# Masking the diagonal block of a stick-breaking attention: a product that adds -1e30 on the matrix engine, or an affine selection on GpSimd

## The chip, the cores and the metric

The kernel runs on one core of one Trainium2 chip. The metric is the device time of one execution in microseconds; lower is better. Times in the profile are microseconds unless ns is written.

## What is computed

One layer on 1024 tokens of width 1024: a norm, one wide projection, two branches (stick-breaking attention with 8 heads of 64, and an RWKV-7 time mix), a gated merge, an output projection and a SwiGLU feed-forward. The change is in the attention, whose reference is, cut to what matters:

```python
for i in range(S // 128):                       # blocks of 128 queries
    z = einsum(q_block, k[:kv_len]) * scale     # kv_len = (i + 1) * 128
    strict = s_idx < t_idx                      # a query sees earlier tokens only
    log_fail = where(strict, log_sigmoid(-z), 0.0)
    after = cumsum(log_fail, reverse=True) - log_fail
    w = where(strict, exp(log_sigmoid(z) + after), 0.0)
    out = w @ v[:kv_len]
```

In numbers rather than logarithms: nb = sigmoid(-z) is the chance that a key does not take the stick, and it counts as 1 where the mask forbids the key. The running product of nb from the last key backwards is what the kernel calls its scan; differences of that product are the weights w.

## The kernel before, in words

Nothing in the code says in which order an engine works. Each operation is recorded with an estimated cost, and a list scheduler in Python (`schedule`) then plays the program through with these costs and fixed latencies between engines, gives out buffers, and writes one order per engine. On the chip each engine works through its order and waits on semaphores. All instructions carry the line L528, the line that issues them, so the profile is read by the names of tiles. The scheduler prefers steps of the running stage and fills holes in TensorE's order with "filler": the projections of the next pair of heads and the gate projections (`gate_tiles`), whose products are named d_d<-big_h. Its cost of a GpSimd operation without an entry of its own is 150 + 2.1 ns per element of a partition; that of the mask's product is 107 ns.

The attention works on 4 pairs p of heads, 2 heads h in each, and 4 double blocks j of two query rows (s = 0, 1), so on 64 rows of 128 queries. A row (`head`) goes through these steps:

- TensorE: for each piece of up to 512 keys two products into a PSUM tile e_e, keys times the high part of the queries (e_e<-b_kst,b_qst) and times the low part (e_e<-b_kst,b_ql). In the piece that ends on the diagonal a third product stands between them: identity times mask in bf16 (e_e<-bf_bf,bf_bf), which adds -1e30 where a key is not earlier than the query. Every product first loads its 128 columns of weights (PEld rows).
- ScalarE (ACT): the sigmoid of the piece, b_nb<-e_e.
- VectorE (DVE): one scan over the whole row, b_nb<-b_nb, 128 to 1024 elements wide.
- TensorE: transposes of the 128x128 blocks of the scanned row (c_c<-cst_cst,b_nb); ScalarE and VectorE split them into b_wt; then the products with the values (y_y<-b_wt,b_vhl), and ScalarE and VectorE finish the head's output (q_q, b_osb).

GpSimd (POOL) has little to do in this stage: for each pair, two MEMSETs of b_ql, and for the values COPYs of a few columns and two TENSOR_TENSORs (b_vt). After the attention come the last gate projections, then the merge (`merge`), whose first products are d_d<-b_orw.

Of the kernel before, what the change touches and what calls it, by code (L numbers as in the profile page):

```python
# [8 lines left out]
BF16 = mybir.dt.bfloat16  # L9
AF = mybir.ActivationFunctionType  # L10
ALU = mybir.AluOpType
# [4 lines left out]
P = 128  # L16
# [21 lines left out]

PC_BG, PC_MU, PC_W0, PC_A0, PC_KK, PC_KA, PC_RK, PC_LW, PC_LB, PC_N = 0, 16, 30, 34, 38, 42, 46, 50, 54, 58

CC_ID, CC_CEN, CC_ONE, CC_MA, CC_DM, CC_TI, CC_SC, CC_N = 0, 128, 256, 384, 512, 640, 896, 1408

# [546 lines left out]
def hybrid_block(tc, x, w_in, consts, params, rows, ups, gup, w_sb, w_rw, w_o, w_fg, w_fu, w_fd, out):  # L591
    b = Block(tc, {a.tensor.name for a in (x, w_in, consts, params, rows, ups, gup, w_sb, w_rw, w_o, w_fg, w_fu, w_fd)})
    nc = b
    T = b.t
    with ExitStack() as es:
        b.open(es)
        b.cls("cst", 1, CC_DM)
        b.cls("par", 1, PC_N)
        b.cls("small", 3, 16)
        b.cls("tiny", 4, 4)  # L600
        b.cls("ss", 8, 4)
        b.cls("carry", 5, 1)
        b.cls("pl", 3, 8)
        b.cls("bf", 2, P)
        b.cls("sp", 3, CH)
        b.cls("q", 4, 256)
        b.cls("big", 4, 4 * S)
        for n in ("raw", "whi", "wlo"):
            b.cls(n, 2, S)
        b.cls("b", NB, 1040, halves=True)  # L610
        for n, k in (("d", 2), ("e", 2), ("c", 2), ("y", 2)):
            b.cls(n, k, H, psum=True)

        cst, par = T("cst", [P, CC_DM]), T("par", [P, PC_N])
        b.xin = []
        for m in range(8):
            b.xin.append(T("b", [P, D], F32, "x"))
            nc.sync.dma_start(b.xin[m], x[m * P : m * P + P, :])
            if m == 0:
                nc.sync.dma_start(cst, consts[:, 0:CC_DM])  # L620
                b.gbc = T("b", [P, D])
                nc.sync.dma_start(b.gbc, rows[0:1, :].broadcast_to([P, D]))
            if m == 3:
                b.w_lora = [b.load(w_in[24], [P, KT, P])]
                nc.sync.dma_start(par, params)
            if m == 5:
                b.w_lora.append(b.load(w_in[25], [P, KT, P]))
        b.ident = cst[:, CC_ID : CC_ID + P]
        b.cen = cst[:, CC_CEN : CC_CEN + P]
        b.ones = cst[:, CC_ONE : CC_ONE + P]  # L630
        b.mask_a = cst[:, CC_MA : CC_MA + P]
        b.tinit = consts[:, CC_TI : CC_TI + 256]
        b.scanm = consts[:, CC_SC:CC_N]
        b.eps = T("small", [P, 2])
        nc.gpsimd.memset(b.eps[:, 0:1], RMS_EPS)
        nc.gpsimd.memset(b.eps[:, 1:2], GN_EPS)
        b.identb = T("bf", [P, P], BF16)
        nc.gpsimd.tensor_copy(b.identb, b.ident)
        b.dmask = T("bf", [P, P], BF16)
        dm = T("q", [P, P])  # L640
        nc.sync.dma_start(dm, consts[:, CC_DM : CC_DM + P])
        nc.gpsimd.tensor_copy(b.dmask, dm)
        b.om = T("small", [P, 14])
        nc.gpsimd.tensor_scalar(out=b.om, in0=par[:, PC_MU : PC_MU + 14], scalar1=-1.0, scalar2=1.0, op0=ALU.mult, op1=ALU.add)
        b.oka = T("small", [P, 4])
        nc.gpsimd.tensor_scalar(out=b.oka, in0=par[:, PC_KA : PC_KA + 4], scalar1=-1.0, scalar2=1.0, op0=ALU.mult, op1=ALU.add)
        b.pc = lambda col: par[:, col : col + 1]

        b.gsc = [b.scratch([P, S], f"gsc{j}") for j in range(16)]
        b.orw_d = [b.scratch([P, S], f"orw{p}") for p in range(PAIRS)]  # L650
        b.x2_d = b.scratch([S, D], "x2d")
        b.w_in, b.w_sb, b.w_rw = w_in, w_sb, w_rw
        b.ngate = 0

        b.steady = STEADY[0]
        norm_in(b)
        lora(b, ups, gup)
        b.steady = STEADY[1]
        rwkv(b)
        b.steady = STEADY[2]  # L660
        attention(b)
        b.steady = STEADY[3]
        merge(b)
        b.steady = True
        output(b, x, w_o, rows)
        ffn(b, w_fg, w_fu, w_fd, rows, out)
        b.issue()


def norm_in(b):  # L670
    nc = b.nc
    T = b.t
    b.hT = tuple([T("big", [P, 4, S], F32R, "h") for q in range(2)] for i in range(2))
    b.table("natural_log_exp_and_others")
    def scale(m):
        xs = T("b", [P, D], F32, "xs")
        return xs, b.rstd([b.xin[m]], xs)

    ahead = [scale(0), scale(1)]
    for m in range(8):  # L680
        xs, r = ahead.pop(0)
        nc.vector.scalar_tensor_tensor(out=xs, in0=b.xin[m], scalar=r, in1=b.gbc, op0=ALU.mult, op1=ALU.mult)
        if m + 2 < 8:
            ahead.append(scale(m + 2))
        b.to_channels(("e", "c"), xs, m, b.hT)
        if m in (2, 4):
            w = b.w_lora[m // 2 - 1]
            hi, lo = T("b", [P, KT, P], F32R), T("b", [P, KT, P], F32R)
            nc.scalar.copy(hi, w)
            nc.gpsimd.tensor_tensor(out=lo, in0=w, in1=hi, op=ALU.subtract)  # L690
            b.w_lora[m // 2 - 1] = hi, lo
# [432 lines left out]
def head(b, kst, qst, ql, vhl, ends, h, j, oh, ol):  # L1124

    nc = b.nc
    T = b.t
    rs = slice(h * CH, h * CH + CH)  # L1130
    nb2 = 2 * j + 2
    wh, wl = ([T("b", [P, min(4, nb2 - 4 * g), 256], F32R, "wt") for g in range((nb2 + 3) // 4)] for _ in range(2))
    for s in range(2):
        i = 2 * j + s
        kv = (i + 1) * P
        qs = slice(i * P, i * P + P)
        nb = T("b", [P, S], F32, "nb")
        for c0 in range(0, kv, H):
            n = min(H, kv - c0)
            z = T("e", [P, H])  # L1140
            ks = slice(c0, c0 + n)
            diag = c0 + n == kv
            nc.tensor.matmul(z[:, :n], lhsT=qst[:, qs], rhs=kst[:, ks], start=True, stop=False)
            if diag:
                nc.tensor.matmul(z[:, n - P : n], lhsT=b.identb, rhs=b.dmask, start=False, stop=False, skip_group_check=True)
            nc.tensor.matmul(z[:, :n], lhsT=ql[:, qs], rhs=kst[:, ks], start=False, stop=True)
            nc.scalar.activation(nb[:, ks], z[:, :n], AF.Sigmoid, scale=-0.125)
        rev = nb[:, 0:kv][:, ::-1]
        nc.vector.tensor_tensor_scan(out=rev, data0=rev, data1=rev, initial=1.0, op0=ALU.mult, op1=ALU.bypass)
        for b0 in range(0, i + 1, 4):  # L1150
            nblk = min(4, i + 1 - b0)
            tp = T("c", [P, 4, P])
            for q in range(nblk):
                nc.tensor.transpose(tp[:, q, :], nb[:, (b0 + q) * P : (b0 + q + 1) * P], b.ident)
            dsl = (slice(None), slice(0, nblk), slice(s * P, s * P + P))
            b.split(wh[b0 // 4][dsl], wl[b0 // 4][dsl], tp[:, :nblk, :])
    o = T("y", [P, 256])
    for kb in range(nb2 - 1, -1, -1):
        first, last = kb == nb2 - 1, kb == 0
        cs = slice(P, 256) if first else slice(0, 256)  # L1160
        g, k = kb // 4, kb % 4
        pairs = [(o[:, cs], vhl[g][:, k, h].rearrange("p a c -> p (a c)"), wh[g][:, k, cs])]
        pairs.append((o[0:CH, cs], vhl[g][:, k, h, 0, :], wl[g][:, k, cs]))
        for n, (out, v, w) in enumerate(pairs if first else reversed(pairs)):
            nc.tensor.matmul(out, lhsT=v, rhs=w, start=first and n == 0, stop=last and n == 1, skip_group_check=True)
    ob = T("q", [P, 256])
    for s in range(2):
        ss = slice(s * P, s * P + P)
        nc.scalar.activation(ob[rs, ss], o[CH:P, ss], AF.Identity, bias=ends[rs, 2 * j + s : 2 * j + s + 1])
    nc.vector.tensor_tensor(out=ob[rs, :], in0=ob[rs, :], in1=o[0:CH, :], op=ALU.add)  # L1170
    osl = slice(j * 256, j * 256 + 256)
    b.split(oh[rs, osl], ol[rs, osl], ob[rs, :])
# [348 lines left out]
def layout(i):  # L1521
# [6 lines left out]
    def cols(v):  # L1528
# [12 lines left out]
        np.eye(P) - blk / CH,  # L1541
        blk,
        np.concatenate([s[:, None] < t[None], s[:, None] <= t[None]], 1),
        np.where(np.arange(P)[None, :] >= np.arange(P)[:, None], -1e30, 0.0),
        (np.arange(32)[None, None, :] == 4 * np.arange(8)[None, :, None] + lane).reshape(P, 256),
        np.broadcast_to(np.arange(H)[None] % CH > 0, (P, H)),
    ]
# [28 lines left out]
```

## Time and profile before

| | |
|---|---|
| median of 3 runs | 1660.45 us (1658.56 to 1661.47) |
| the profiled execution's own time | 1659.71 us |
| its span in the trace | 1657.9 us |
| TensorE busy | 1603.0 us, 97% of the span |
| VectorE, ScalarE, GpSimd busy | 68%, 43%, 12% |
| attention in the trace | from about 541 us (first scan) to 787 us (last product with the values) |

The span is what the trace shows from its first to its last instruction; 1.8 us of the execution's own time lie around it. A busy share is an average over stages with different limits.

### The profile page before, as it was taken

The page shows a single profiled execution, that of the slowest core. Times are in us where ns is not written, and L with a number is a line of the kernel's source. Part 1 is how long each engine was busy: PE and PEld are TensorE (multiplying, and loading weights), DVE is VectorE, ACT ScalarE, POOL GpSimd, SP SyncE. Part 2 cuts the span into 40 slices and gives each one's busy share as a digit, 9 for nine tenths or more (in the row PEclk, how much of TensorE's full clock was granted, in tenths as well). Part 3 has the DMA queues.
Part 4 walks back from the last instruction along what each step waited for, and adds up shares of the span by engine and source line. Part 5 has one row for each costly group of instructions (what it writes and reads, how often), then busy time and mean ns, then how long its engine had stood idle before and what let it go on. Part 6 is the DMA issues. An engine that isn't in the chain of part 4 may idle for free.

```text
span 1657.9 us, 23575 instructions
## 1 busy us (share of the span) xinstructions
PE 1603.0 (97%) x8876; PEld 1273.8 (77%) x8876; DVE 1124.1 (68%) x1999; ACT 718.0 (43%) x1403; POOL 206.6 (12%) x344
## 2 busy tenths in 40 slices
PE   6999999999999999999999999999999999999998
PEld 5777776776777777777787788888888888888886
DVE  6567789668784877878248446766666666778484
ACT  7532334433334656566433434333233322455352
POOL 2021232512313010000015120000000000000000
PEclk9999999999999999999999999999999999999999
DMA  6533222242320000001644501233332332774455
GB/s 217 201 88 91 78 80 79 75 137 72 99 77 34 32 26 14 26 26 39 214 135 142 195 39 58 89 96 106 110 107 97 127 95 96 276 270 141 137 167 178
DMA packets 107108, 180.96 MB, mean 109 GB/s; under 512 B 42353, under 2 KB 43505, under 8 KB 106993
## 3 DMA queue, kind: packets, MB, share of 16 engines
q1 hardware_dynamic: 106992, 179.44, 33.1%
q8 instruction: 70, 1.15, 0.3%
q14 instruction: 46, 0.37, 0.1%
HBM read 129.86 MB, written 47.45 MB: 107 GB/s over the span
## 4 chain that ended last, share of the span: by engine, by line
PE 74%; DVE 17%; ACT 4%; issue 3%; DMA 2%; POOL 0%; SPq 0%; DVEq 0%; ACTq 0%; POOLq 0%
PE d_d L528 31%; PE e_e L528 17%; PE c_c L528 15%; PE y_y L528 10%; DVE q_q L528 6%; DVE b_nb L528 3%; ACT b_qst L528 1%; DVE b_wt L528 1%; DVE wlo_wlo L528 1%; DVE b_sv L528 1%; ACT whi_whi L528 1%; DVE b_nx L528 1%; ACT b_wt L528 1%; DVE b_kst L528 1%; DMA b_b<-rows 0%
## 5 line engine op out<-in xcount | busy, mean ns | idle before, releaser
L528 PE MATMUL d_d<-big_h,whi_whi 128*128 128x512 f32 x1280 | 431.5, 408 | 3.7 <-DVE b_kst L528 2.8
L528 PEld LDWEIGHTS d_d<-big_h,whi_whi 128*128 128x128 f32 x1280 | 234.7, 189 | 52.0 <-issue 6.3
L528 PE MATMUL d_d<-big_h,wlo_wlo 128*128 128x512 f32 x640 | 260.3, 407 | 0.0
L528 PEld LDWEIGHTS d_d<-big_h,wlo_wlo 128*128 128x128 f32 x640 | 120.7, 189 | 24.0 <-issue 1.9
L528 DVE TENSOR_TENSOR wlo_wlo<-raw_raw,whi_whi 128x1024 fp32r<-128x1024 f32 (+1 forms) x60 | 70.6, 1177 | 40.0 <-ACT whi_whi L528 38.6
L528 ACT CAST whi_whi<-raw_raw 128x1024 fp32r<-128x1024 f32 (+1 forms) x60 | 55.9, 933 | 92.5 <-PE d_d L528 82.5
L528 DVE TENSOR_TENSOR q_q<-b_nl,q_q 128x2 f32<-128x2 f32 (+30 forms) x248 | 85.6, 345 | 11.0 <-PE y_y L528 2.7
L528 DVE TENSOR_TENSOR_SCAN b_nb<-b_nb 128x128 f32<-128x128 f32 (+3 forms) x64 | 87.5, 1395 | 1.0
L528 POOL TENSOR_SCALAR sp_sp<-b_sv,pl_pl 64x64 f32<-64x64 f32 x120 | 58.1, 485 | 117.7 <-DVE b_sv L528 110.8
L528 DVE TENSOR_REDUCE q_q<-q_q 128x1 f32<-128x2 f32 (+30 forms) x248 | 62.1, 250 | 6.7
L528 PE MATMUL d_d<-b_wd,big_act 128*128 128x512 f32 x264 | 66.6, 395 | 0.0
L528 PE MATMUL e_e<-b_wd,big_act 128*128 128x512 f32 x264 | 66.6, 394 | 0.0
L528 ACT CAST b_wd<-b_wraw 128x512 fp32r<-128x512 f32 x71 | 42.2, 620 | 53.2 <-DVE b_wraw L528 22.7
L528 DVE TENSOR_TENSOR b_wd<-b_wraw,b_wd 128x512 fp32r<-128x512 f32 x71 | 46.7, 686 | 23.4 <-ACT b_wd L528 23.4
L528 PEld LDWEIGHTS d_d<-b_wd,big_act 128*128 128x128 f32 x264 | 49.6, 188 | 11.8
L528 PEld LDWEIGHTS e_e<-b_wd,big_act 128*128 128x128 f32 x264 | 49.6, 188 | 11.8
L528 PE MATMUL c_c<-cst_cst,b_nb 128*128 128x128 f32 x288 | 47.9, 280 | 9.2 <-DVE b_wt L528 4.5
L528 ACT COPY b_xv<-c_c 64x64 f32<-64x64 f32 x64 | 13.3, 208 | 92.1 <-DVE b_xv L528 46.6
L528 ACT CAST b_wt<-c_c 128x512 fp32r<-128x512 f32 (+2 forms) x96 | 43.9, 481 | 21.0 <-PE c_c L528 19.9
L528 DVE TENSOR_TENSOR b_wt<-c_c,b_wt 128x512 fp32r<-128x512 f32 (+2 forms) x96 | 50.0, 547 | 4.5 <-ACT b_wt L528 3.8
L528 PEld LDWEIGHTS c_c<-cst_cst,b_nb 128*128 128x128 f32 x288 | 32.6, 140 | 23.9 <-DVE b_wt L528 12.2
L528 PE MATMUL c_c<-b_wd,big_act 128*128 128x512 f32 x198 | 50.6, 395 | 0.0
(651 smaller groups left out, 3558.0 us busy)
## 6 DMA issues: line engine op xcount, KB each, us to landing
raw_raw<-w_in SPq DMA_DIRECT2D x42, 512.0 KB, 3.4
raw_raw<-w_fg SPq DMA_DIRECT2D x22, 512.0 KB, 3.5
raw_raw<-w_fu SPq DMA_DIRECT2D x22, 512.0 KB, 4.0
b_wraw<-w_fd SPq DMA_DIRECT2D x22, 512.0 KB, 5.0
act<-b_u SPq DMA_DIRECT2D x40, 256.0 KB, 3.4
b_x<-x SPq DMA_DIRECT2D x16, 512.0 KB, 6.3
raw_araw<-act SPq DMA_DIRECT2D x14, 512.0 KB, 4.3
whi_araw<-act SPq DMA_DIRECT2D x14, 512.0 KB, 4.9
```

Of the source, the lines that this page charges most:

```text
L528: getattr(getattr(self.real, op.engine), op.method)(**kw)
```

## The change: what it does

The third product is gone, and with it the mask tile, the bf16 identity, the two conversions and the transfer that made them at the start, and the columns of the constants that held the mask. Instead, after the sigmoids of a row, GpSimd runs one AFFINE_SELECT in place on the diagonal block of b_nb (128x128, float32): it keeps an element where query minus key is positive and writes 1.0 elsewhere. The scan of the row now waits for it.

```diff
-            diag = c0 + n == kv
             nc.tensor.matmul(z[:, :n], lhsT=qst[:, qs], rhs=kst[:, ks], start=True, stop=False)
-            if diag:
-                nc.tensor.matmul(z[:, n - P : n], lhsT=b.identb, rhs=b.dmask, start=False, stop=False, skip_group_check=True)
             nc.tensor.matmul(z[:, :n], lhsT=ql[:, qs], rhs=kst[:, ks], start=False, stop=True)
             nc.scalar.activation(nb[:, ks], z[:, :n], AF.Sigmoid, scale=-0.125)
+
+        own = nb[:, kv - P : kv]
+        nc.gpsimd.affine_select(out=own, in_=own, pattern=[[-1, P]], compare_op=ALU.is_gt, fill=1.0, base=0, channel_multiplier=1)
         rev = nb[:, 0:kv][:, ::-1]
         nc.vector.tensor_tensor_scan(out=rev, data0=rev, data1=rev, initial=1.0, op0=ALU.mult, op1=ALU.bypass)
...
-        b.identb = T("bf", [P, P], BF16)
-        nc.gpsimd.tensor_copy(b.identb, b.ident)
-        b.dmask = T("bf", [P, P], BF16)
-        dm = T("q", [P, P])
-        nc.sync.dma_start(dm, consts[:, CC_DM : CC_DM + P])
-        nc.gpsimd.tensor_copy(b.dmask, dm)
```

The scheduler is not touched, but it plays a different program, so the orders change between the attention's first score products and its last product with the values. Ahead of that stretch TensorE's order is the same, and behind it too, but for the number of filler products in between.

GpSimd's order at the start of the attention, before. The sp_sp are the last of the RWKV chain, b_r the last output of that branch, b_ql the low part of the queries of pair 1, pl_pl and b_vt the values of pair 1:

```order
L528 COPY pl_pl_5328<-b_tmp_3453 128x4
L528 TENSOR_TENSOR b_v_2529<-b_tmp_3453 128x512
L528 TENSOR_TENSOR b_r_2433<-b_r_2433 128x512
L528 MEMSET b_ql_5671 64x1024
L528 MEMSET b_ql_5673 64x1024
L528 MEMSET b_vt_5883 128x1
L528 COPY pl_pl_5991<-b_vt_5883 128x4
L528 TENSOR_TENSOR b_vt_5883<-b_vt_5883 128x512
```

and the same place now, from the same two rows on:

```order
L528 TENSOR_TENSOR b_v_2523<-b_tmp_3447 128x512
L528 TENSOR_TENSOR b_r_2427<-b_r_2427 128x512
L528 AFFINE_SELECT b_nb_5517<-b_nb_5517 128x128
L528 AFFINE_SELECT b_nb_5520<-b_nb_5520 128x128
L528 AFFINE_SELECT b_nb_5570<-b_nb_5570 128x128
L528 AFFINE_SELECT b_nb_5576<-b_nb_5576 128x128
L528 AFFINE_SELECT b_nb_5597<-b_nb_5597 128x128
L528 AFFINE_SELECT b_nb_5639<-b_nb_5639 128x128
L528 MEMSET b_ql_5671 64x1024
L528 MEMSET b_ql_5673 64x1024
L528 AFFINE_SELECT b_nb_5688<-b_nb_5688 128x128
L528 AFFINE_SELECT b_nb_5718<-b_nb_5718 128x128
```

The selections of the first rows stand directly behind the TENSOR_TENSOR on b_r, and the MEMSETs of b_ql have moved behind six of them.

TensorE's order in pair 0, second head, from just behind the score products of the row of 384 keys down to the transposes of that row, before (the 384-key row is b_nb_6547; d_d_6507 is filler):

```order
L528 MATMUL e_e_6544<-b_kst_5492,b_qst_5776 128x512
L528 LDWEIGHTS bf_bf_145
L528 MATMUL e_e_6544<-bf_bf_294,bf_bf_145 128x128
L528 MATMUL c_c_6549<-cst_cst_136,b_nb_6531 128x128
L528 MATMUL e_e_6544<-b_kst_5492,b_ql_5673 128x512
L528 MATMUL c_c_6552<-cst_cst_136,b_nb_6535 128x128 x2
L528 MATMUL d_d_6507<-big_h_186,wlo_wlo_6253 128x512
L528 MATMUL e_e_6563<-b_kst_5492,b_qst_5776 128x512
L528 MATMUL e_e_6563<-b_kst_5492,b_ql_5673 128x512
L528 MATMUL d_d_6507<-big_h_186,whi_whi_6241 128x512
L528 MATMUL e_e_6571<-b_kst_5492,b_qst_5776 128x128
L528 MATMUL c_c_6575<-cst_cst_136,b_nb_6547 128x128 x2
```

and now, from the same place on; the row of 384 keys is b_nb_6585 here, and its first transpose stands behind two more products of 512 columns (one filler, one score product) that follow the last row shown:

```order
L528 MATMUL e_e_6581<-b_kst_5486,b_qst_5745 128x512
L528 MATMUL e_e_6581<-b_kst_5486,b_ql_5673 128x512
L528 MATMUL d_d_6528<-big_h_167,whi_whi_6266 128x512
L528 MATMUL c_c_6590<-cst_cst_136,b_nb_6563 128x128
L528 MATMUL d_d_6528<-big_h_173,whi_whi_6266 128x512
L528 MATMUL e_e_6598<-b_kst_5486,b_qst_5745 128x512
L528 MATMUL e_e_6598<-b_kst_5486,b_ql_5673 128x512
L528 MATMUL c_c_6605<-cst_cst_136,b_nb_6566 128x128 x2
L528 MATMUL e_e_6612<-b_kst_5486,b_qst_5745 128x128
L528 MATMUL e_e_6612<-b_kst_5486,b_ql_5673 128x128
L528 MATMUL d_d_6528<-big_h_167,wlo_wlo_6279 128x512
L528 MATMUL d_d_6528<-big_h_184,whi_whi_6266 128x512
```

The mask product and its weight load are gone, and more filler stands between a row's scores and its transposes. At the start of the attention the four score products of the rows of 384 and 512 keys now stand directly in front of the first row's transpose; before, they stood behind it. In return less filler is left for the end: between the last product with the values and the first d_d<-b_orw stood 96 products d_d<-big_h, and now 75.

## Rows read from the trace of the kernel before

**Rows 1.** The page: span; busy time, share and instructions of each engine; and TensorE's busy share in 40 slices.

```profile
span 1657.9 us, 23575 instructions
PE 1603.0 (97%) x8876; PEld 1273.8 (77%) x8876; DVE 1124.1 (68%) x1999; ACT 718.0 (43%) x1403; POOL 206.6 (12%) x344
PE   6999999999999999999999999999999999999998
```

**Rows 2.** Two stretches, the attention and all that follows: length, busy time of PE, PEld, DVE, ACT and POOL (instructions), granted clock of TensorE as a share of full speed, DMA share, GB/s.

```profile
541.00:787.00 246.00, 231.58 (x1354) 183.27 (x1353) 190.14 (x262) 152.59 (x345) 16.54 (x25) 1.00 0.08 27
787.00:1658.00 871.00, 861.56 (x3745) 696.82 (x3743) 550.23 (x788) 330.38 (x578) 46.15 (x24) 1.00 0.41 137
```

**Rows 3.** What TensorE waited for between 535 and 790 us: us in total, times, longest; the three longest of five.

```profile
PE c_c L528 <- DVE b_wt L528: 4.5, 10, 1.0
PE c_c L528 <- DVE b_nb L528: 3.6, 5, 0.9
PE e_e L528 <- ACT b_nb L528: 2.2, 3, 0.8
```

**Rows 4.** The same, from 785 us to the end, all of it.

```profile
PE e_e L528 <- ACT b_woh L528: 1.3, 2, 1.1
PE d_d L528 <- DVE b_g L528: 0.8, 1, 0.8
PE e_e L528 <- DVE b_wol L528: 0.7, 1, 0.7
```

**Rows 5.** TensorE in order of time: start, us, operation, x instructions merged into the row, idle time before it. Products overlap, so what one costs is the time from its start to the next start.

```profile
598.51 0.66 PE L528 MATMUL c_c<-cst_cst,b_nb 128*128 128x128 f32 x4 [0.80 <-DVE b_nb L528]
598.93 0.31 PE L528 MATMUL e_e<-b_kst,b_qst 128*128 128x128 f32 x1
...
611.58 0.63 PE L528 MATMUL d_d<-big_h,whi_whi 128*128 128x512 f32 x2
612.05 0.39 PE L528 MATMUL d_d<-big_h,wlo_wlo 128*128 128x512 f32 x1
...
613.44 0.40 PE L528 MATMUL e_e<-b_kst,b_qst 128*128 128x512 f32 x1
613.68 0.23 PE L528 MATMUL e_e<-bf_bf,bf_bf 128*128 128x128 bf16 x1
613.72 0.48 PE L528 MATMUL e_e<-b_kst,b_ql 128*128 128x512 f32 x1
614.04 0.63 PE L528 MATMUL d_d<-big_h,whi_whi 128*128 128x512 f32 x2
...
615.89 0.39 PE L528 MATMUL e_e<-b_kst,b_qst 128*128 128x512 f32 x1
616.12 0.40 PE L528 MATMUL e_e<-b_kst,b_ql 128*128 128x512 f32 x1
616.36 0.22 PE L528 MATMUL e_e<-b_kst,b_qst 128*128 128x128 f32 x1
616.42 0.23 PE L528 MATMUL e_e<-bf_bf,bf_bf 128*128 128x128 bf16 x1
616.46 0.31 PE L528 MATMUL e_e<-b_kst,b_ql 128*128 128x128 f32 x1
616.60 0.45 PE L528 MATMUL d_d<-big_h,wlo_wlo 128*128 128x512 f32 x1
```

**Rows 6.** The mask products as a group: shapes, count, busy time, mean ns of one, idle time before them.

```profile
L528 PE MATMUL e_e<-bf_bf,bf_bf 128*128 128x128 bf16 x64 | 14.6, 228 | 0.0
```

**Rows 7.** Groups of GpSimd's instructions, same columns.

```profile
L528 POOL TENSOR_SCALAR sp_sp<-b_sv,pl_pl 64x64 f32<-64x64 f32 x120 | 58.1, 485 | 117.7 <-DVE b_sv L528 110.8 <-DVE q_q L528 1.1
L528 POOL TENSOR_TENSOR b_vt<-b_vt 128x512 f32<-128x512 f32 x6 | 6.2, 1040 | 0.0
L528 POOL COPY b_sm<-carry_carry 128x1 f32<-128x1 f32 x3 | 0.6, 185 | 0.2
L528 POOL CAST bf_bf<-q_q 128x128 bf16<-128x128 f32 x1 | 0.3, 292 | 2.1 <-DMA q_q<-consts 2.1
```

**Rows 8.** ScalarE, and then GpSimd, in order of time around 585 us: a GpSimd instruction that waited for ScalarE.

```profile
584.55 0.59 ACT L528 COPY b_vt<-d_d 128x512 f32<-128x512 f32 x1
...
585.20 0.19 POOL L528 COPY pl_pl<-b_vt 128x4 f32<-128x4 f32 x1 [23.59 <-ACT b_vt L528]
```

**Rows 9.** VectorE and GpSimd in order of time where they met, from 594 us, and VectorE at 624 us, where GpSimd was idle.

```profile
594.30 1.23 DVE L528 TENSOR_TENSOR wlo_wlo<-raw_raw,whi_whi 128x1024 fp32r<-128x1024 f32 x1 [1.69 <-ACT whi_whi L528]
595.67 2.79 DVE L528 TENSOR_TENSOR_SCAN b_nb<-b_nb 128x896 f32<-128x896 f32 x1
...
594.81 0.76 POOL L528 COPY pl_pl<-b_vt 128x4 f32<-128x4 f32 x1 [8.29 <-ACT b_vt L528]
595.54 1.04 POOL L528 TENSOR_TENSOR b_vt<-b_vt 128x512 f32<-128x512 f32 x1
...
624.42 2.03 DVE L528 TENSOR_TENSOR_SCAN b_nb<-b_nb 128x896 f32<-128x896 f32 x1
```

**Rows 10.** The first two rows of the attention: ScalarE's sigmoids, VectorE's scans, GpSimd, and TensorE's first transpose, in order of time on each engine.

```profile
540.74 0.55 ACT L528 ACTIVATE b_nb<-e_e 128x128 f32<-128x128 f32 x2
...
541.22 2.06 DVE L528 TENSOR_TENSOR_SCAN b_nb<-b_nb 128x128 f32<-128x128 f32 x2
...
541.44 1.30 POOL L528 TENSOR_TENSOR b_r<-b_r 128x512 f32<-128x512 f32 x1 [10.07 <-issue]
...
542.04 0.27 PE L528 MATMUL c_c<-cst_cst,b_nb 128*128 128x128 f32 x1
```

**Rows 11.** The chain of work that ended last, behind the attention's last product: start, us, instructions of TensorE merged.

```profile
787.30 20.83 PE d_d L528 x90
```

More of the change, by code (lines that the diff above doesn't have):

```diff
@@ L39 @@
 PC_BG, PC_MU, PC_W0, PC_A0, PC_KK, PC_KA, PC_RK, PC_LW, PC_LB, PC_N = 0, 16, 30, 34, 38, 42, 46, 50, 54, 58
-CC_ID, CC_CEN, CC_ONE, CC_MA, CC_DM, CC_TI, CC_SC, CC_N = 0, 128, 256, 384, 512, 640, 896, 1408
+CC_ID, CC_CEN, CC_ONE, CC_MA, CC_TI, CC_SC, CC_N = 0, 128, 256, 384, 512, 768, 1280
 ENGINES = ("tensor", "vector", "scalar", "gpsimd", "sync")
@@ L596, in hybrid_block @@
         b.open(es)
-        b.cls("cst", 1, CC_DM)
+        b.cls("cst", 1, CC_TI)
         b.cls("par", 1, PC_N)
@@ L603, in hybrid_block @@
         b.cls("pl", 3, 8)
-        b.cls("bf", 2, P)
         b.cls("sp", 3, CH)
@@ L612, in hybrid_block @@
             b.cls(n, k, H, psum=True)
-        cst, par = T("cst", [P, CC_DM]), T("par", [P, PC_N])
+        cst, par = T("cst", [P, CC_TI]), T("par", [P, PC_N])
         b.xin = []
@@ L619, in hybrid_block @@
             if m == 0:
-                nc.sync.dma_start(cst, consts[:, 0:CC_DM])
+                nc.sync.dma_start(cst, consts[:, 0:CC_TI])
                 b.gbc = T("b", [P, D])
@@ L1543, in layout @@
         np.concatenate([s[:, None] < t[None], s[:, None] <= t[None]], 1),
-        np.where(np.arange(P)[None, :] >= np.arange(P)[:, None], -1e30, 0.0),
         (np.arange(32)[None, None, :] == 4 * np.arange(8)[None, :, None] + lane).reshape(P, 256),
```

## The prediction

> **What bounds the kernel now.** I read the page first: TensorE is busy 97% of the span, and after the first slice no slice is under 90% until the last [rows 1]. So the sum is made on TensorE, and other engines count where they keep it waiting. The next view is the stretches: in the attention TensorE is busy 231.58 of 246.00 us, which leaves 14.4 us idle, while VectorE is busy 190.14 and GpSimd 16.54; behind the attention it is busy 861.56 of 871.00 us [rows 2]. The clock is granted in full in both, so it is no term. The waits say that the idle time in the attention comes mostly from VectorE: 4.5 us for the splitting of transposed blocks and 3.6 us for the scans, and 2.2 us for ScalarE's sigmoids [rows 3]. Behind the attention only 2.8 us of waits are left [rows 4]: whatever TensorE gains there is carried to the end, since the last gate projections follow without a hole for 20.83 us [rows 11], and the order behind them is the same as before.
>
> **What the removed product costs.** The group's busy time, 14.6 us for 64 at 228 ns [rows 6], is no price, because products overlap. What counts is the distance between starts [rows 5]. A masked piece of 512 keys runs from 613.44 to 614.04, 0.60 us; an unmasked one from 615.89 to 616.36, 0.47 us. The mask thus costs 0.13 us: 0.04 us until the next product starts, and the rest in that product, which needs 0.32 us instead of 0.24. The 128-key row says the same in another way: mask 0.04 us (616.42 to 616.46) and the product behind it 0.14 us, where the 128-column product in front of it took 0.06; that makes 0.04 + 0.08 = 0.12 us. I take 0.125 us, 64 times: **8.0 us** of TensorE's time. The bounds: 64 x 0.04 = 2.6 us if the product behind it does not get faster, and the 14.6 us of the group.
>
> **What the set-up costs.** Two conversions of 0.29 us on GpSimd and one transfer of 64 KB go. GpSimd waited 2.1 us in front of the second conversion [rows 7], so it was not late; I take nothing, and with that cover gone it would be 0.6 us at most.
>
> **What the selection costs.** The trace has no such instruction. The row of the same size and with one input is the conversion of 128x128, 0.29 us [rows 7]; a COPY of one column takes 0.185 us, so about 0.19 us is fixed and 0.8 ns goes to each element. The upper end is the TENSOR_TENSOR of 128x512 with two inputs, 1.04 us; between them lies a TENSOR_SCALAR of 64x64 at 0.485 us, which shares the compute with a scalar from memory. I take 0.4 us: size and input count are those of the conversion, and a comparison comes on top. The way there: GpSimd started at 585.20 behind a ScalarE instruction that ended at 585.14, 0.06 us [rows 8]; I take about the same from GpSimd to VectorE, which no row shows. A row's chain from sigmoid to scan thus gets 0.06 + 0.4 + 0.06 = 0.5 us longer where nothing is in the way.
>
> **What covers it.** In the new order more work of TensorE stands between a row's last score product and its first transpose. Take the place shown. Before: three 512-column score products without a mask in between and one with it, two fillers, three transposes, one 128-column product. Now: four 512-column score products, a fifth one, five fillers and three transposes, and two 128-column products. With 0.235 us for 512 columns (611.58 to 612.05 holds two), 0.105 for a transpose (598.51 to 598.93 holds four) and 0.06 for 128 columns [rows 5], that is 4 x 0.235 + 0.125 + 2 x 0.235 + 3 x 0.105 + 0.06 = 1.9 us before and 5 x 0.235 + 5 x 0.235 + 3 x 0.105 + 2 x 0.06 = 2.8 us now, 0.9 us more. The chain of 0.5 us fits into it with 0.4 us to spare. The filler that does this is work that stood behind the attention: 96 products there before, 75 now. The sum of TensorE's work does not change by it.
>
> **What is not covered.** First, the two engines block each other. GpSimd's COPY of 4 columns took 0.76 us instead of 0.19 while VectorE ran a TENSOR_TENSOR from SBUF, and ended with it at about 595.55; the scan of 896 behind it took 2.79 us instead of 2.03 beside GpSimd's TENSOR_TENSOR [rows 9]. So a selection waits for a scan that is running, and the next scan for the selection. Where two scans follow each other in VectorE's order, as they mostly do in runs of two or three, VectorE stands still for some 0.5 us. [...] All of it on VectorE is 64 x 0.5 = 32 us of its 56 us idle time in the stage (246.00 - 190.14, [rows 2]). TensorE sees of this only what exceeds the spare 0.4 us; I take one row in ten, six rows, 0.1 us late each, 0.6 us in all, and keep 0.1 us in every row, 6.4 us, as the bound. Second, GpSimd's queue. The first selections stand behind the TENSOR_TENSOR on b_r, which ends at 542.74, while the first two sigmoids end at 541.29 and the first scan started at 541.22 [rows 10]: the first scan starts at about 542.74 + 0.4 + 0.06 = 543.2, ends 0.4 later, and the first transpose, at 542.04 before, can start at 543.7, 1.7 us later. The new order has four score products in front of that transpose which stood behind it, 4 x 0.22 = 0.9 us: what is left is 0.8 us of new wait, once. At the other three places where the values' TENSOR_TENSOR stands in front of a selection, the scan already waited for it in the run before (2.79 against 2.03), so nothing is new.
>
> **The sum.** -8.0 + 0.6 + 0.8 = -6.6 us. The profiled execution took 1659.71 us of its own, so it would take 1653.1; the median of the runs shown stands 0.7 us above it, and from there it is 1660.45 - 6.6 = 1653.9, rounded **1654.0 us**, a factor of 0.996.
>
> **The rivals.**
>
> *The gain is eaten by the blocking.* Nothing else differs, but each row costs TensorE 0.1 us in waits: -8.0 + 6.4 + 0.8 = -0.8, 1659.7 us. For it: TensorE's waits for VectorE are the main idle time already, and VectorE's runs of scans have no gaps. Against it: the new order moved the transposes back by about twice the selection's chain.
>
> *VectorE becomes the bound: slower.* If a selection takes as long as the TENSOR_TENSOR row, 1.04 us, and each holds VectorE up for its length, VectorE needs 190.14 + 64 x 1.04 = 256.7 us for a stretch of 246.00: 10.7 us more than now, 1671 us. It decides from 56/64 = 0.87 us of standstill a row on. For it: the rows 9 show that the holding is real in both directions; a slow selection needs only 2.2 times my price. Against it: GpSimd's one-input rows of this size are at 0.29 us.
>
> [...]
>
> *The mask's product was free.* If TensorE's time behind the mask was set by waits for VectorE anyway, the 8.0 us turn into more waiting and the time stays at 1660.4. For it: 14.4 us of idle time in this stretch. Against it: 93% busy, and filler without dependences that moves up.
>
> **How the numbers follow.** Runs of this kernel differ by 2.9 us, so I call 0.2%, 3.3 us, what a measurement can tell from no change: faster means below 1657.1, slower above 1663.8. The forecast has 0.62, with a range of its own of 1650 to 1656.5 (a price of 0.15 us a mask with the first wait alone gives -9.6 + 0.8, 1651.7, and up to 2 of the 3.6 us of waits for scans may go with the transposes moved back; 0.05 us a row in waits gives -8.0 + 3.2 + 0.8, 1656.4). The eaten gain has 0.11, VectorE as the bound 0.14, the fetched code 0.07, the free product 0.06. Faster gets 0.63, taking in a small part of the eaten gain; the same 0.21, of the eaten gain, the fetched code and the free product; slower 0.16, with a little of the eaten gain beyond 0.15 us a row. The range of 8 in 10 is 1649.5 to 1662: it leaves out VectorE as the bound and a few hundredths at either end.
>
> **What would show it.** Right: 8812 products of TensorE instead of 8876, the product behind the place of the mask at 0.24 us (512) and 0.06 us (128), selections of 0.3 to 0.5 us, and the first d_d<-b_orw about 6 us earlier than before. Waits of TensorE for the scans and the splits together no longer than before by more than 2 us. Wrong: selections near 1 us, or many rows in which VectorE waits for GpSimd with TensorE waiting for that scan; a stall of several us before the first selection; or a merge that starts earlier and then waits for its gates, whose transfer is on the chain.

## The result, and the profile after

The changed kernel takes 1648.99 us (median of 6 runs, 1646.55 to 1650.92), the kernel before 1660.35 (6 runs). The ratio is 0.9933 [0.9923, 0.9943], that is -11.1 us. The direction of the forecast came true; the gain is 4.5 us larger than its sum of -6.6, and the median lies 0.5 us under the low end of its range.

The page of the kernel after, the lines that answer to [rows 1]: span, and busy time of each engine. 64 products are gone, GpSimd works 40 us longer.

```profile
span 1644.8 us, 23649 instructions
PE 1594.3 (97%) x8812; PEld 1272.7 (77%) x8812; DVE 1121.3 (68%) x1999; ACT 717.7 (44%) x1403; POOL 246.8 (15%) x406
```

For a comparison that holds for several kernels I take one stretch: from the start of the attention's first sigmoid to the start of the first d_d<-b_orw, that is the attention and the rest of the gate products. It starts at the same place of the program in every kernel, though not at the same time. Columns as in [rows 2]. First before, then after:

```profile
540.74:809.30 268.56, 254.14 (x1452) 201.64 (x1451) 196.84 (x269) 161.22 (x357) 16.54 (x25) 1.00 0.11 36
```

```profile
538.88:798.50 259.62, 245.02 (x1391) 199.26 (x1390) 194.44 (x269) 161.06 (x357) 58.79 (x89) 1.00 0.11 37
```

The spans of the two profiled executions differ by 13.1 us (the one after is the fastest of its six), and 8.9 of them lie in this stretch. 1.9 us lie ahead of it, and the change did not make them: kernels of the experiments below without the old set-up reached the first sigmoid anywhere from 538.7 to 543.9 us. 2.3 us lie behind it, where 1.3 us of TensorE's waits are left after, against the 2.8 of [rows 4]; the length of that part too varies by more than this from kernel to kernel (846.1 to 849.3 us). The waits behind the stretch after:

```profile
PE e_e L528 <- DVE b_wol L528: 0.7, 1, 0.7
PE d_d L528 <- ACT b_mg L528: 0.4, 1, 0.4
PE e_e L528 <- ACT b_woh L528: 0.2, 1, 0.2
```

In the stretch TensorE's busy time fell by 9.1 us; its idle time did not move: 14.4 us before (268.56 - 254.14), 14.6 after. What it waited for did move. The waits of TensorE in the attention after, the four longest, to be read against [rows 3]:

```profile
PE c_c L528 <- DVE b_wt L528: 6.3, 11, 1.3
PE y_y L528 <- DVE b_wt L528: 3.2, 6, 0.8
PE c_c L528 <- DVE b_vhl L528: 2.2, 3, 0.8
PE c_c L528 <- DVE b_nb L528: 1.4, 6, 0.4
```

Before, the row of y_y behind VectorE's splits, which [rows 3] leave out, was:

```profile
PE y_y L528 <- DVE b_wt L528: 0.9, 2, 0.5
```

The waits for the scans (b_nb) fell from 3.6 to 1.4 us, those for the splits on VectorE (b_wt, in front of c_c and y_y together) rose from 5.4 to 9.5. How much of that is the new order and how much the selections, two kernels below tell apart. VectorE itself waited for the selections little, 7.7 us in all:

```profile
DVE b_nb L528 <- POOL b_nb L528: 7.7, 5, 2.1
```

TensorE in order of time after, a masked piece of 512 keys (starts at 611.68) and one of 128 (612.14), columns as in [rows 5]:

```profile
611.68 0.40 PE L528 MATMUL e_e<-b_kst,b_qst 128*128 128x512 f32 x1
611.91 0.39 PE L528 MATMUL e_e<-b_kst,b_ql 128*128 128x512 f32 x1
612.14 0.22 PE L528 MATMUL e_e<-b_kst,b_qst 128*128 128x128 f32 x1
612.20 0.27 PE L528 MATMUL e_e<-b_kst,b_ql 128*128 128x128 f32 x1
612.31 0.45 PE L528 MATMUL d_d<-big_h,wlo_wlo 128*128 128x512 f32 x1
```

The product behind the mask's place needs 0.23 us until the next start instead of 0.32, and the whole piece 0.46 (611.68 to 612.14) instead of 0.60. The 128-key piece takes 0.17 us, where it took 0.24 (616.36 to 616.60). That is 0.14 and 0.07 us less; the forecast had 0.13 and 0.12.

The selections as a group on GpSimd, and, in order of time, one that met no scan and one beside a long scan with that scan (VectorE):

```profile
L528 POOL TENSOR_SCALAR_AFFINE_SELECT b_nb<-b_nb 128x128 f32<-128x128 f32 x64 | 41.2, 653 | 132.1 <-ACT b_nb L528 130.1 <-DVE b_osb L528 1.3 <-DVE b_nb L528 0.6
```

```profile
544.46 0.29 POOL L528 TENSOR_SCALAR_AFFINE_SELECT b_nb<-b_nb 128x128 f32<-128x128 f32 x1 [3.12 <-ACT b_nb L528]
```

```profile
594.75 2.27 POOL L528 TENSOR_SCALAR_AFFINE_SELECT b_nb<-b_nb 128x128 f32<-128x128 f32 x1
...
594.58 2.35 DVE L528 TENSOR_TENSOR_SCAN b_nb<-b_nb 128x1024 f32<-128x1024 f32 x1
```

Alone, with no scan beside it, it took 0.29 us: 283 to 295 ns in 28 of the 30 that met no scan. The mean of 653 ns is made by 24 of the 64 that take over 0.35 us; 22 of these end 0.09 us (86 to 95 ns) behind the end of a scan.

### The profile page after: what moved, and what is told of

It is laid out like the page before. It is cut to its first block, busy times and chain, and to the rows that moved or that the text cites. A ratio compares the mean times of both kernels' runs of the same rounds, so it can differ in the third digit from the quotient of the medians.

```text
span 1644.8 us, 23649 instructions
## 1 busy us (share of the span) xinstructions
PE 1594.3 (97%) x8812; PEld 1272.7 (77%) x8812; DVE 1121.3 (68%) x1999; ACT 717.7 (44%) x1403; POOL 246.8 (15%) x406
## 4 chain that ended last, share of the span: by engine, by line
PE 73%; DVE 16%; issue 5%; ACT 2%; DMA 2%; POOL 1%; SPq 0%; DVEq 0%; POOLq 0%; ACTq 0%
PE d_d L528 31%; PE e_e L528 17%; PE c_c L528 16%; PE y_y L528 10%; DVE q_q L528 6%; DVE b_nb L528 3%; DVE b_wt L528 1%; DVE wlo_wlo L528 1%; DVE b_sv L528 1%; DVE b_nx L528 1%; POOL b_nb L528 1%; ACT b_qst L528 1%; ACT whi_whi L528 0%; DMA b_b<-rows 0%; DVE b_bk L528 0%
## 5 line engine op out<-in xcount | busy, mean ns | idle before, releaser
L528 PE MATMUL d_d<-big_h,whi_whi 128*128 128x512 f32 x1280 | 435.9, 410 | 3.8 <-DVE b_kst L528 2.8
L528 POOL TENSOR_SCALAR_AFFINE_SELECT b_nb<-b_nb 128x128 f32<-128x128 f32 x64 | 41.2, 653 | 132.1 <-ACT b_nb L528 130.1
```

The lines of the kernel that those rows point to most:

```text
L528: getattr(getattr(self.real, op.engine), op.method)(**kw)
```

## The experiments

A difference below is the ratio to the kernel before, taken of 1660 us; one between two experiments is uncertain by 2 to 3 us. Where the scheduler plays a changed program, it plans a new order too, also where the text names only the instruction that changed.

**The old set-up kept in the changed kernel.** The conversions and the transfer are back, nothing uses them.

```diff
+        b.identb = T("bf", [P, P], BF16)
+        nc.gpsimd.tensor_copy(b.identb, b.ident)
+        b.dmask = T("bf", [P, P], BF16)
...
+        nc.gpsimd.tensor_copy(b.dmask, dm)
```

> The changed kernel with the old set-up left in: the transfer of the mask and the two conversions to bf16 still run at the start, and nothing reads them. Theory A (the gain is TensorE's time behind the 64 mask products, the set-up is hidden): 1648 to 1650.5 us, as the changed kernel. Rival B (the set-up delays the first stage and is worth 1 to 2 us of the 11.4): 1650.5 to 1651.5 us, and the first sigmoid of the attention as late as before the change.

1648.28 us, 0.9931 [0.9917, 0.9944], -11.5 us: as the changed kernel without it. The set-up costs nothing.

**Neither mask nor selection.** The two lines of the selection are taken out of the changed kernel.

> The changed kernel without the selection: the attention is not masked at all, neither by a product nor by a selection; the rest is computed. Theory A (the selection is covered by the filler that the scheduler moves in front of the transposes): 1647.5 to 1650 us, within 1.5 us of the changed kernel. Rival C (the selection has a hidden price that the mask's product more than paid for): 1643 to 1646 us.

1652.72 us, 0.9955 [0.9941, 0.9968], -7.5 us: 3.6 us slower than the kernel that does the selection as well. That lies outside both expected ranges. Less work and more time: the order must carry something, because without the selection's cost the scheduler plans the transposes 0.69 us earlier.

**Both.** The selection is added to the kernel before.

> The kernel before with the selection added on top: both mask product and selection. Theory A (the selection is free, the mask costs 0.12 to 0.14 us a row): 1659.5 to 1661.5 us, as before. Rival C (the selection has a price): 1663 us or more. Rival D (part of the gain is the new order that the selection brings, not the product that goes): 1655 to 1658 us.

1657.51 us, 0.9988 [0.9979, 0.9997], -2.0 us, as rival D had it: an instruction added for nothing makes the kernel no slower. From here to the changed kernel it is another -9.1 us, by the mask's product.

**The mask's product twice** in the kernel before.

```diff
+                nc.tensor.matmul(z[:, n - P : n], lhsT=b.identb, rhs=b.dmask, start=False, stop=False, skip_group_check=True)
```

> The kernel before with every mask product issued twice, so 64 products of 128 columns more. Theory A (each mask costs TensorE 0.12 to 0.14 us that is carried to the end): 1667.5 to 1669.5 us if the second costs what the first does; at least 1663 us if a second product behind a first costs only its own 0.04 us. Rival E (the product hides behind waits for VectorE): 1660 to 1662 us.

1663.03 us, 1.0017 [1.0008, 1.0025], +2.8 us, 0.04 us each. TensorE in order of time in this kernel:

```profile
615.23 0.29 PE L528 MATMUL e_e<-bf_bf,bf_bf 128*128 128x128 bf16 x2
615.33 0.48 PE L528 MATMUL e_e<-b_kst,b_ql 128*128 128x512 f32 x1
615.64 0.40 PE L528 MATMUL d_d<-big_h,whi_whi 128*128 128x512 f32 x1
```

Both together take 0.10 us of slots, and the product behind them 0.31 us, as behind one (0.32 [rows 5]). So doubling shows only the slot of one product; the slowing of the product behind it is paid once. A doubled piece does not give the price of the first.

**The plan does not see the selection.** In the changed kernel the scheduler's cost of the selection is set so that the planned way from sigmoid to scan is as long as in the kernel before.

```diff
+        if method == "affine_select":
+            return -270.0
```

> The changed kernel, but the scheduler is told that the selection takes no time at all between sigmoid and scan, so that it orders as if there were none. Theory F (the selection itself is not free; what pays for it is the order, in which the scheduler moves a row's transposes back by its planned 0.69 us): at least the 1652.7 us of the kernel without mask and selection, 1652.5 to 1657 us. Rival G (the order has nothing to do with it): 1647.5 to 1650 us, as the changed kernel.

1659.68 us, 0.9998 [0.9989, 1.0007], -0.3 us. The same instructions as in the changed kernel, in an order that leaves no room for the selection: 10.8 us slower than it, and slower than either theory had it. Waits of TensorE and of VectorE in the attention of this kernel:

```profile
PE c_c L530 <- DVE b_wt L530: 9.1, 17, 1.5
PE c_c L530 <- DVE b_nb L530: 4.4, 8, 0.9
...
DVE b_nb L530 <- POOL b_nb L530: 6.8, 7, 1.9
```

VectorE waits for selections no longer than after (6.8 and 7.7 us); TensorE waits more, for what comes from VectorE. What differs is the order. Against the kernel with neither, which is planned just as early, the selection here costs 7.2 us (-7.5 to -0.3), 0.11 us a row.

**The order alone, with the mask, and without mask and selection.** In both the scheduler believes that a scan can start 0.69 us later than it does, which is what it plans for the selection (419 ns and 270 of latencies). The first is otherwise the kernel before, the second the changed kernel without its selection.

```diff
-            q.ready = max(q.ready, op.end + wait(e, q.engine))
+            late = 689.0 * (q.kw["op1"] == ALU.bypass) if e == "scalar" and q.method == "tensor_tensor_scan" else 0.0
+            q.ready = max(q.ready, op.end + wait(e, q.engine) + late)
```

> The kernel before, mask product and all, with only the scheduler told that a scan can start 0.69 us later after its sigmoid. Theory F: 1656 to 1658.5 us, as the kernel with both mask and selection (1657.5). Rival G: 1659 to 1661 us.

> Neither mask product nor selection on the chip (the attention is not masked), but the scheduler is told that a scan can start 0.69 us later after its sigmoid, as long as it planned for the selection. Theory F (the order alone brings it): 1646 to 1649.5 us, 3 to 6 us under the 1652.7 of the same program without that delay in the plan. Rival G (what made the kernel with the selection faster than the one without lies in the selection on the chip): 1652 to 1654 us.

With the mask 1654.78 us, 0.9966 [0.9953, 0.9978], -5.6 us; without both 1645.38, 0.9908 [0.9894, 0.9921], -15.3 us. Both gain more than expected, and rival G is excluded. The same stretch as above, from the first sigmoid to the first d_d<-b_orw, of the first and of the second:

```profile
540.93:804.70 263.77, 250.96 (x1453) 201.77 (x1452) 196.59 (x269) 162.12 (x357) 19.00 (x25) 1.00 0.12 37
```

```profile
538.71:793.50 254.79, 244.65 (x1391) 199.56 (x1390) 195.63 (x269) 161.43 (x357) 18.07 (x25) 1.00 0.12 38
```

This makes a path from before to after in three steps, each with one thing changed in the program. Between the second kernel and after, TensorE's order is almost the same: 124 of its 8812 places hold another product, by the names of tiles and shapes. Between the first and the second it is not (924 places, the mask's products left out), so the step of the mask carries a new order as well.

| step | by the ratios | length of the stretch | TensorE's idle time in it | busy time |
|---|---|---|---|---|
| order alone (before, first) | -5.6 | -4.8 | 14.4 to 12.8 | -3.2 |
| mask's product off (first, second) | -9.7 | -9.0 | 12.8 to 10.1 | -6.3 |
| selection on (second, after) | +4.2 | +4.8 | 10.1 to 14.6 | +0.4 |
| sum | -11.1 | -8.9 | +0.2 | -9.1 |

The unmoved idle time of the result is thus two moves that cancel: order and mask take 4.3 us of it away, the selection puts 4.5 back. The waits for scans and splits, in the first kernel:

```profile
PE c_c L529 <- DVE b_wt L529: 8.3, 12, 1.2
PE c_c L529 <- DVE b_nb L529: 1.6, 6, 0.4
PE y_y L529 <- DVE b_wt L529: 1.0, 3, 0.4
```

and in the second:

```profile
PE c_c L529 <- DVE b_wt L529: 5.4, 9, 1.2
PE c_c L529 <- DVE b_nb L529: 1.5, 4, 0.5
PE y_y L529 <- DVE b_wt L529: 1.5, 3, 0.8
```

So it is the order that turned waits for scans into waits for splits: the first kernel has no selection. What the selection adds is 2.6 us in front of the splits (6.9 to 9.5) and the 2.2 us for b_vhl, which the second does not have.

Without the mask's product the same order is worth 7.8 us (-7.5 to -15.3), and with the selection on the chip 10.8 (-0.3 to -11.1).

**The selection over the whole row**, 128 to 1024 columns instead of 128, planned at the same 419 ns, so that only its length on the chip grows.

```diff
-        own = nb[:, kv - P : kv]
+        own = nb[:, 0:kv]
...
-... pattern=[[-1, P]], ... base=0, ...
+... pattern=[[-1, kv]], ... base=kv - P, ...
```

> The changed kernel with the selection run over the whole row of 128 to 1024 keys instead of its last 128, with the scheduler told the old cost, so that TensorE's order is the same row by row. On the chip each selection takes 0.1 to 0.8 us longer (some 0.36 us on average by 0.8 ns an element), 23 us in all. Theory A (selections of this size are covered by the order): 1648 to 1651 us. Theory C (the selection holds the scan up and TensorE sees part of it): 1653 to 1662 us.

1665.48 us, 1.0034 [1.0021, 1.0046], +5.6 us, 16.7 over the changed kernel, 0.26 us a row, and above both expected ranges. TensorE's order is that of the changed kernel, product by product. Its selections of 1024 columns on GpSimd, and what VectorE and TensorE waited for:

```profile
L530 POOL TENSOR_SCALAR_AFFINE_SELECT b_nb<-b_nb 128x1024 f32<-128x1024 f32 x8 | 15.1, 1886 | 9.1 <-ACT b_nb L530 8.9
```

```profile
DVE b_nb L530 <- POOL b_nb L530: 13.2, 9, 2.6
...
PE c_c L530 <- DVE b_wt L530: 10.7, 15, 2.3
PE y_y L530 <- DVE b_wt L530: 5.2, 7, 2.1
PE c_c L530 <- DVE b_nb L530: 5.0, 6, 1.7
```

So the mechanism of the slower rival exists and has a dose: with the longer selections VectorE's waits for them rose from 7.7 us (after) to 13.2, and TensorE's waits for scans and splits from 10.9 to 20.9. At 0.29 us the dose is small. The 64 selections of this kernel take 66.6 us together, 1.04 each, which is the price that the rival assumes. It came to 1665.5 us and not to 1671: VectorE was not the bound, with 201.55 us busy in the 261.00 us from 541 to 802 us.

**A scheduler that knows how long a scan takes.** If another order is worth 5.6 us by itself, the old plan was wrong about something. The scheduler costs the scan at 68 + 1.042 ns per element, 1135 ns for 1024. The scans of the kernel before in the attention, as groups by shape:

```profile
L528 DVE TENSOR_TENSOR_SCAN b_nb<-b_nb 128x1024 f32<-128x1024 f32 x8 | 18.2, 2271 | 0.0
L528 DVE TENSOR_TENSOR_SCAN b_nb<-b_nb 128x128 f32<-128x128 f32 x8 | 3.3, 416 | 0.1
```

That is 2271 ns for 1024, and (2271 - 416) / 896 = 2.07 ns per element. Three kernels got this cost: the changed one (with 290 ns for the selection), the kernel before, and the one with neither mask nor selection.

```diff
+        if method == "tensor_tensor_scan" and kw["op1"] == ALU.bypass:
+            return 150 + 2.07 * n
...
+        if method == "affine_select":
+            return 290.0
```

> The changed kernel, with two of the scheduler's costs set from the rows: the attention's scan at 150 + 2.07 ns an element (rows: 416 ns for 128, 2271 for 1024; the scheduler had 68 + 1.04) and the selection at 290 ns. Theory F (the order before put the transposes too early, since the scheduler takes a scan for half as long as it is): 1644 to 1648 us, better than the changed kernel. Rival G: 1648 to 1651 us.

> The kernel before, mask product and all, with the scheduler's cost of the attention's scan corrected to 150 + 2.07 ns an element. Theory F (the wrong cost of the scan is most of TensorE's idle time; the mask costs TensorE 0.11 to 0.14 us a row in any order): 1633 to 1639 us, some 20 to 27 us under the kernel before, and 5 to 9 us above the corrected kernel with the selection (1628.8). Rival H (in a right order the mask hides in what is left of the waits, and product and selection cost the same): 1627 to 1631 us.

> Neither mask product nor selection on the chip (the attention is not masked), with the scheduler's cost of the scan corrected. Theory F with a selection that costs 3 us as in the old orders: 1624 to 1627 us. If in a right order the selection is covered in full: 1627.5 to 1630 us, as the corrected kernel with the selection (1628.8).

The changed kernel: 1628.82 us, 0.9813 [0.98, 0.9827], -31.0, some 15 us more than was expected. With the mask: 1639.0, 0.9872 [0.9858, 0.9885], -21.2. With neither: 1631.15, 0.9827 [0.9814, 0.984], -28.7, above both expected ranges. The first has the lowest median of all. Its stretch from the first sigmoid to the first d_d<-b_orw, all that TensorE waited for in the attention, and its selections:

```profile
543.73:782.30 238.57, 237.65 (x1390) 202.53 (x1389) 197.43 (x269) 159.15 (x357) 65.83 (x89) 1.00 0.12 41
```

```profile
PE c_c L532 <- DVE b_nb L532: 0.9, 3, 0.5
```

```profile
L532 POOL TENSOR_SCALAR_AFFINE_SELECT b_nb<-b_nb 128x128 f32<-128x128 f32 x64 | 46.9, 738 | 115.7 <-ACT b_nb L532 115.5
```

Of 14.6 us idle time 0.9 is left, and the stretch is 21.1 us shorter than after. With a plan that fits the chip better, taking the mask's product out still gives 7.5 us (21.2 against 28.7), and replacing it by the selection 9.8 (21.2 against 31.0). The kernel with the selection is no slower than the one without (31.0 against 28.7). That is no price of the selection by itself, since the two plans differ by its planned delay; no run takes it out of this order. But all of TensorE's recorded waits are 0.9 us here, though a selection still takes 738 ns on the mean.

## Why the prediction was right in direction and too small

**The mask's product, -8.0: right.** Four comparisons give -7.5 (before to neither), -9.1 (both to after), -9.7 (order alone) and -7.5 (corrected plan), 0.12 to 0.15 us each, a new order included. In the step that removes it the busy time of the stretch falls by 6.3 us, 0.10 for each of the 62 mask products in it; the other 2.7 are idle time. The rows of two pieces above say 0.14 and 0.07. The distance between starts was the right row; the busy time of the group, 14.6 us, was not the price, nor was the bare slot, 2.6.

**The set-up, 0: right** (-11.5 with it, -11.1 without).

**The selection itself: right place, price a little high.** 0.29 us alone, the conversion's row, against the 0.4 taken; its way is 0.07 us after ScalarE and 0.03 before VectorE.

**The order: here the prediction failed.** The step reads "The sum of TensorE's work does not change by it" and uses the 0.9 us of work between scores and transposes as cover for the selection, and as nothing else. But the cover was worth something before there was anything to cover: the order alone gives -5.6 us, and -7.8 where there is neither mask nor selection. The rows to see it were there: TensorE's 8.1 us of waits for scans and splits [rows 3], and a scan of 896 at 2.03 us [rows 9], which the scheduler's formula puts at 68 + 1.042 x 896 = 1.00. I let "up to 2 of the 3.6 us of waits for scans" go with it in the range of the likeliest case, and gave the sum none of it. In the trace of before a scan of 1024 took 2.27 us on the mean (the group above), where a TENSOR_TENSOR of 1024 on VectorE took 1.23 [rows 9].

**The new waits, +1.4: too small.** They are +4.2 us here (+3.6 on the kernel with the mask, from order alone to both; +7.2 in the order that leaves no room). Of the two terms, the 0.8 us at the head of GpSimd's queue did not come. The first rows after on ScalarE, GpSimd, VectorE and TensorE, to be read against [rows 10]:

```profile
538.88 0.56 ACT L528 ACTIVATE b_nb<-e_e 128x128 f32<-128x128 f32 x2
...
539.58 1.28 POOL L528 TENSOR_TENSOR b_r<-b_r 128x512 f32<-128x512 f32 x1 [9.86 <-issue]
540.82 0.53 POOL L528 TENSOR_SCALAR_AFFINE_SELECT b_nb<-b_nb 128x128 f32<-128x128 f32 x2
...
541.14 1.07 DVE L528 TENSOR_TENSOR_SCAN b_nb<-b_nb 128x128 f32<-128x128 f32 x2 [1.69 <-POOL b_nb L528]
...
541.34 0.34 PE L528 MATMUL e_e<-b_kst,b_qst 128*128 128x384 f32 x1
541.52 0.34 PE L528 MATMUL e_e<-b_kst,b_ql 128*128 128x384 f32 x1
541.69 0.39 PE L528 MATMUL e_e<-b_kst,b_qst 128*128 128x512 f32 x1
541.92 0.39 PE L528 MATMUL e_e<-b_kst,b_ql 128*128 128x512 f32 x1
542.15 0.27 PE L528 MATMUL c_c<-cst_cst,b_nb 128*128 128x128 f32 x1
542.18 0.71 PE L528 MATMUL d_d<-big_h,whi_whi 128*128 128x512 f32 x2
542.73 0.38 PE L528 MATMUL c_c<-cst_cst,b_nb 128*128 128x128 f32 x2
```

Times are to be counted from the first sigmoid here, since this execution reached it 1.9 us earlier. The TENSOR_TENSOR on b_r starts 0.70 us behind it, as before. The queue is as forecast: the first scan starts 2.26 us behind the sigmoid instead of 0.48, 1.8 us later (forecast: 1.7). But the first transpose stands 2.0 us later too (3.27 instead of 1.30), with no wait in front of it: besides the four score products (0.8 us) the new order has 1.2 us more filler there, which the prediction did not count. So the 4.2 us belong to the rows, 0.07 us each, where I had 0.6 us in all and kept 0.1 us a row as the bound; how much of it is the blocking and how much the longer chain itself, the runs do not separate. -5.6 us that the sum left out, +2.8 that it put too low and -1.7 on the mask make the difference of -4.5. That the median lies only 0.5 us outside the range is in part luck: two misses of opposite sign.

**The range** ended at 1649.5 because its lower end held a higher price of the mask and a few waits, but no gain from the order.

**The rivals.** The gain eaten by blocking: its mechanism is there at two thirds of its size, but it met a larger gain. It comes true in full where the plan leaves no room: 0.11 us a row there, and -0.3 us in all. VectorE as the bound: it is busy 194.44 of 259.62 us; no. Its dose showed with the selection over the whole row only, and below its price. The fetched code, at 0.07: no run shows such a time. The first two selections begin where the TENSOR_TENSOR on b_r ends (540.82 and 539.58 + 1.28 = 540.86) and take 0.53 us together, with no stall between. The free product: excluded, it is the largest term (the "93% busy" against it is 94%, 231.58 of 246.00).

**What would show it.** The 8812 products came as written, and 0.23 us behind the mask's place of 512 keys; behind that of 128 keys it was 0.11 us instead of 0.06 (612.20 to 612.31). The selections took 0.29 us alone, as forecast, but 0.65 on the mean. The first d_d<-b_orw came 10.8 us earlier instead of 6, 8.9 counted from the first sigmoid. Waits for scans and splits rose by 1.9 us ([rows 3] 8.1, with the 0.9 behind y_y 9.0; after 10.9), just inside the 2 us that I had called right, and still hid a loss of 4 us. The kernels between tell it apart: 10.9 with the order alone, 8.4 with the mask's product off, 10.9 with the selection on. A sum of waits before and after cannot separate such moves.

**Open:** of the 4.8 us that the order alone takes from the stretch only 1.6 are recorded as idle time of TensorE; 3.2 are busy time, at the same products. From after to the corrected plan it is 13.7 of 21.1. One wait can be seen to lie in part inside the recorded busy time. In TensorE's order of time before:

```profile
542.07 0.48 PE L528 MATMUL d_d<-big_h,whi_whi 128*128 128x512 f32 x1
543.43 0.41 PE L528 MATMUL c_c<-cst_cst,b_nb 128*128 128x128 f32 x2 [0.87 <-DVE b_nb L528]
```

The product at 542.07 stands behind a transpose and counts as busy for 0.48 us. Where nothing waits, the first of two such products takes about 0.32 to the next start (542.18 to 542.73 after, 0.55 for two, less 0.23 for the second). So this wait of some 1.0 us is recorded as 0.87, 0.16 short. The corrected kernel has 26 waits fewer than after (3 against 29), which at 0.16 us each is, as an estimate, 4 of its 7.4 us. It does not explain the order alone, with 24 waits against 23; that stays open. Nor is it shown that the gain of the order lies in the later transposes alone: the orders differ in other places too.

## What to carry to other kernels

Where a scheduler plans with costs, a new instruction changes the plan as well as the work: split the two by giving the old program the new order, and the new program the old one. Compare every cost in the plan with its row in the trace before costing an edit: here one wrong line (the scan) was worth more (-20 to -21 us) than the edit (-11), and with it put right the kernel with the selection is no slower than the one without. Compare stretches from a place in the program and not from a time: the same place came up to 5 us apart in these executions. Price a short product by the distance between the starts around it, not by its busy time and not by issuing it twice: here 0.07 to 0.14 us, against 0.23 and 0.04.

## What the runs showed of the hardware

- Of the 24 GpSimd selections that started beside a running VectorE scan after, 23 ended 0.09 us (86 to 95 ns) behind the end of a scan: 0.29 us alone, 2.27 us beside a scan of 1024, and 0.653 us on the mean. The scans were hardly lengthened by it (2.30 us on the mean for 1024 columns after, 2.27 before); the hold in the other direction is shown by the TENSOR_TENSOR of [rows 9] alone, beside which a scan of 896 took 2.79 us instead of 2.03. That the cost depends on the plan I had not expected: 0.11 us a row of TensorE's time where the plan leaves no room, 0.07 in the changed kernel, and 0.9 us of waits in all once the plan fitted.
- A second 128-column bf16 product behind a first cost 0.04 us by the time and 0.06 by the rows, the first with the slowing of the float32 product behind it 0.07 to 0.14 by the rows and 0.12 to 0.15 by the time, the new order included.
